# Operands of products at 0 modulo 256, taps for alike placement, and the conditioning dots as one task

## The chip, the cores and the metric

One core of a Trainium2 chip. The time is that of one execution of the program on the device, in microseconds (us); of several runs the median is given. Engines: TensorE (PE) multiplies matrices, VectorE (DVE), ScalarE (ACT) and GpSimd (POOL) work elementwise, SyncE (SP) issues most transfers.

## The reference

A decoder trunk of two layers on 1024 tokens with 1024 channels, in float32. Cut to what matters:

```python
c_act = silu(c)
for i in range(2):
    mod = c_act @ ada_w[i] + ada_b[i]                  # 6 vectors of 1024
    sh_m, sc_m, g_m, sh_f, sc_f, g_f = split(mod, 6)
    h = rms_norm(x, norm_mix_g[i]) * (1 + sc_m) + sh_m
    y = conformer_conv(h, ...) if i == 0 else multiscale_pool(h, ...)
    x = x + (1 + g_m) * y
    h = rms_norm(x, norm_ffn_g[i]) * (1 + sc_f) + sh_f
    x = x + (1 + g_f) * ((silu(h @ w_gate) * (h @ w_up)) @ w_down)   # 1024 -> 2816 -> 1024
return rms_norm(x, final_g)
```

conformer_conv is a product 1024 -> 2048, a GLU, a causal depthwise convolution over 31 tokens (per channel), a layer norm, silu, and a product 1024 -> 1024. multiscale_pool takes means over 2, 4, 8 and 16 tokens and small products.

## The kernel before

Channels lie on the 128 partitions, tokens along the free dimension. The 1024 tokens are two chunks of 512, A and B; the 1024 channels are eight tiles k (or p) of 128. A matrix product in full precision is three products in the one-pass type float32r: both operands are split into a high part and a low rest (`hi`, `lo`), and `products` (L423) does hi x hi, lo x hi and hi x lo into one PSUM bank, each a 128x128 weight and a moving operand of 512 columns.

The program interleaves the chunks: convolution on A, on B, feed-forward of layer 0 on A (the taps of B run beside it), the second convolution product on B, feed-forward of layer 0 on B (pooling of A beside it), and so on, with layer 1. The order of the work is made when the program is built: `unit` lists the units of PE's work, and `pace` (L187) lets tasks issue DVE and POOL instructions where an estimated clock of these engines lags PE's; `finish` (L199) issues a task to its end, there and then. Each engine then runs its own instructions strictly in that order.

**Placement.** The moving operands live in tiles of the pool `slots`. `slot` (L239) gives chunk B a tile of 512 columns. For chunk A it gives a tile of 514 and returns it from column 2 on, since the tile also serves as a buffer of the convolution with two columns ahead (`slot_after`, L243). `wslot` (L247) gives 542 columns (30 of the convolution's past, 512 of the chunk); it holds u, the input of the convolution, later the pooling input hp, and `ffn_p1` (L873) takes the pairs ghi and glo from it. The pool's tiles lie 2080 bytes apart for A, 2048 for B and 2176 for the wide ones. The weights w, two planes of 1024 columns, lie 64 bytes past multiples of 256.

**Taps.** Of the 31 taps of the convolution PE does all for the channel tile p = 7 on chunk A and 8 for p = 6 (`PE_TAPS`, `pe_taps`, L636), as products with diagonal weights; tap j needs u moved by 30 - j tokens, and the moving operand begins at another column for odd and for even taps. `split_u` (L628) makes u's high and low part for p = 6. All other taps are DVE's, or POOL's with ACT (class `Taps`, L660): ca sums DVE's part in PSUM, pa POOL's in SBUF, and the last steps put them together. The layer norm of A then sums the tiles into acc, of which PE takes the mean.

**Dots.** The product c_act @ ada_w is done by DVE: one dot is an instruction over 128x1024 that multiplies a loaded tile adaw (0.5 MB) by c_act and sums along the free dimension. An `ada_task` (L324) holds two buffers, loads ahead over SP's queue, and pauses between dots for a time of `LOAD` (L49, in estimated us of PE). The vectors 4 and 5 of layer 0 (scale and gate of the feed-forward) are two such tasks (L1144), started after the layer norm of A; vector 4 is finished (L1147) ahead of the norm that needs it. The 48 dots of layer 1 start at L1158, with the first feed-forward.

Of the kernel before, what the change touches and what calls it, by code (L numbers as in the profile page):

```python
# [16 lines left out]
P = 128  # L17
D = 1024
S = 1024
KT = D // P  # L20
# [6 lines left out]
PHALO = max(WINDOWS) - 1  # L27
EPS = 1e-6
# [20 lines left out]
LOAD = {"load": 4.0, "slow": 18.0, "next": 4.0, "dots": 3.5}  # L49
# [65 lines left out]
def trunk(ctx, tc, xT, c, vec, ada, adan, w1f, w1, wdg, w2, wgu, wdn, wpl, out):  # L115
# [178 lines left out]


# [28 lines left out]
    def ada_task(l, js, pause=None):  # L324
# [250 lines left out]
    def conv_u(ch, p):  # L575
        u = st["u", ch.i, p] = wslot(ch, "u")
        if ch.i == 0:
            G_.memset(u[:, :HALO], 0.0)
        else:
            G_.tensor_copy(u[:, :HALO], uhalo[:, p, :])  # L580
        return u

    def conv_glu(ch, p, ba, bg):
# [3 lines left out]
        if ch.i == 0 and PE_TAPS.get(p) == CW:  # L587

            V_.scalar_tensor_tensor(ba, ba, V("conv_b1", p), sg, op0=ADD, op1=MUL)
            hi, lo = st["us", p] = [slot_after(A, name) for name in ("uhi", "ulo")]  # L590
            for part in (hi, lo):
                G_.memset(part[:, :2].bitcast(F32), 0.0)
            S_.copy(hi[:, 2:], ba)
            V_.tensor_tensor(lo[:, 2:], ba, hi[:, 2:].bitcast(F32), op=SUB)
# [6 lines left out]
    def conv_in(*todo):  # L601

        def emit(take):
            got = {}
            for each in todo:
# [15 lines left out]
                if ch.i == 0 and 0 < PE_TAPS.get(p, 0) < CW:  # L621
                    split_u(p)
                if ch.i == 0 and PE_TAPS.get(p, 0) < CW:
                    T["taps", 0, p] = Taps(A, p, PE_TAPS.get(p, 0))
# [3 lines left out]
    def split_u(p):  # L628


        u = st["u", 0, p][:, HALO - 2 :]
        hi, lo = st["us", p] = [slot_after(A, name) for name in ("uhi", "ulo")]
# [3 lines left out]
    def pe_taps(p):  # L636

        groups = tap_groups(p)
        us = []
        for i, js in enumerate(groups):  # L640
            def emit(take, i=i, js=js):
# [3 lines left out]
                for q, j in enumerate(js):  # L645
                    o = (CW - 1 - j) // 2 * 2
                    i0 = 2 - (CW - 1 - j) % 2
                    products(b[:, o:], wt, q, [v[:, i0 : i0 + A.n - o] for v in st["us", p]], j == CW - 1, j == CW - PE_TAPS[p])
                    if q % 4 == 3:
                        pace()  # L650
                if i == len(groups) - 1:
                    if PE_TAPS[p] == CW:
# [7 lines left out]
    class Taps:  # L660
# [5 lines left out]
        def __init__(self, ch, p, others=0):  # L666
            self.ch, self.p, self.done, self.urgent = ch, p, False, False
            self.next, self.acc, self.part = 0, None, None

            self.end, self.awaits, self.other = CW - max(others, 1), others > 0, None  # L670
            tasks.append(self)

        def step(self, e):
# [6 lines left out]
            if self.next < self.end:  # L680
                if e == "V" and self.acc is None and sum(isinstance(t, Taps) and t.acc is not None for t in tasks) >= 2:
                    return False
                if e == "G":
                    if self.acc is None and self.part is None and sum(isinstance(t, Taps) and t.part is not None for t in tasks) >= 2:
                        return False
                    if self.next >= self.end - 2:
                        return False
                j = self.next
                self.next += 1
# [21 lines left out]
            d = u[:, HALO : HALO + n]  # L711
            if self.awaits:
                if self.part is not None:
                    V_.tensor_tensor(d, self.part, self.acc, op=ADD)
                else:
                    S_.copy(d, self.acc)
                V_.tensor_tensor(d, d, self.other, op=ADD)
            else:
                if self.part is not None:
                    V_.tensor_tensor(self.acc, self.part, self.acc, op=ADD)  # L720
                V_.scalar_tensor_tensor(d, d, w(CW - 1), self.acc, op0=MUL, op1=ADD)
# [85 lines left out]
    def pool_h(ch, l):  # L807

        hp = st["hp", ch.i] = [wslot(ch, "hp") for _ in range(KT)]
# [63 lines left out]
    def ffn_p1(ch, l, f, pick, first):  # L873
        def emit(take):
# [15 lines left out]
            hi, lo = st["g", ch.i, f] = [wslot(ch, name, F32R)[:, : ch.n] for name in ("ghi", "glo")]  # L890
# [248 lines left out]
    unit(lambda take: finish(*(T["taps", 0, p] for p in range(KT) if PE_TAPS.get(p, 0) < CW)))  # L1139
# [120 lines left out]
```

## Time and profile before

| | us |
|---|---|
| median of 3 runs | 1873.54 (1871.35 to 1875.83) |
| profiled execution | 1871.14 |
| its span, first to last instruction | 1869.4 |
| PE busy | 1826.0 (98%) |
| DVE busy | 990.9 (53%) |
| ACT busy | 968.0 (52%) |
| POOL busy | 614.8 (33%) |

A row of the timeline has the start, the time, the engine, the source line, the operation, what it writes and reads, its shape and count, and in brackets the idle time of the engine just before with what ended it. The time of a product contains its latency and overlaps the next one, so what a product costs PE is the distance from its start to the next start. In a table by stage the numbers are the busy time of PE, PE's weight loads, DVE, ACT and POOL with their counts, the clock that was granted to PE (1.00 is full), and the DMA's share and GB/s. Names such as `hhi`, `ghi`, `vhi`, `mxhi` are high parts of the moving operands of gate and up (and of the first convolution product), of dn, of the second convolution product, and of the pooling product.

### The profile page before, as it was taken

How to read it: one execution, taken by the hardware profiler on the slowest of the kernel's cores; microseconds unless marked ns; L12 is line 12 of the kernel's file. 1: busy time of each engine (PE TensorE's matmuls, PEld its weight loads, DVE VectorE, ACT ScalarE, POOL GpSimd, SP SyncE). 2: the span in 40 equal slices, each digit the busy share in tenths (PEclk: the TensorE clock that was granted, in tenths of full speed). 3: DMA queues.
4: the chain of work that ended last, by engine and by line, in shares of the span. 5: the costliest groups of instructions: out<-in, count | busy, mean ns of one | idle time of the engine just before them, and what ended most of it. 6: DMA issues, size and time to landing. Idle time of an engine off the chain costs nothing.

```text
span 1869.4 us, 21783 instructions
## 1 busy us (share of the span) xinstructions
PE 1826.0 (98%) x8085; PEld 1481.9 (79%) x8085; DVE 990.9 (53%) x1528; ACT 968.0 (52%) x1240; POOL 614.8 (33%) x662
## 2 busy tenths in 40 slices
PE   7999998999999999999999999999999999999997
PEld 5777776888888888877888888888888888888886
DVE  8899856988875235585622233734432233322225
ACT  3775665766656454454644445644534454444443
POOL 4587522877733211272111111511111111111111
PEclk9999998999999999999999999999999999999998
DMA  7958797888978987999887878778778879788782
GB/s 289 300 151 221 172 263 222 225 222 208 223 189 216 231 221 185 283 261 269 227 194 178 211 171 205 182 173 205 181 178 196 192 177 250 176 205 197 181 195 68
DMA packets 108285, 387.56 MB, mean 207 GB/s; under 512 B 11793, under 2 KB 13969, under 8 KB 108178
## 3 DMA queue, kind: packets, MB, share of 16 engines
q0 software_dynamic: 44208, 160.98, 47.2%
q1 hardware_dynamic: 62880, 224.13, 34.6%
q8 instruction: 64, 1.05, 0.2%
q10 hardware_dynamic: 1090, 1.05, 0.2%
q14 instruction: 43, 0.35, 0.1%
HBM read 381.92 MB, written 4.19 MB: 207 GB/s over the span
## 4 chain that ended last, share of the span: by engine, by line
PE 82%; DVE 10%; DMA 6%; issue 1%; ACT 1%; SPq 0%; POOL 0%; DVEq 0%
PE gate L131 24%; PE up L131 24%; PE dn L131 24%; DMA adaw<-in_ada_dram 5%; DVE ca L109 4%; PE y L131 4%; PE first L131 3%; DVE adaw L109 1%; DVE acc L109 1%; PE g L131 1%; PE a L131 1%; DVE x L109 1%; DVE t L109 1%; DMA adaw<-in_adan_dram 1%; DVE hlo L109 1%
## 5 line engine op out<-in xcount | busy, mean ns | idle before, releaser
L109 ACT CAST w<-raw 128x1024 fp32r<-128x1024 f32 x317 | 331.0, 1044 | 508.2 <-issue 303.8
L131 PE MATMUL gate<-hhi,w 128*128 128x512 f32 x1408 | 455.4, 393 | 2.3 <-DVE x L109 1.7
L131 PE MATMUL up<-hhi,w 128*128 128x512 f32 x1408 | 455.9, 393 | 0.0
L131 PE MATMUL dn<-ghi,w 128*128 128x512 f32 (+1 forms) x1440 | 445.7, 386 | 1.2 <-DMA w<-in_wdn_dram 1.2
L417 POOL DMA_DIRECT2D w<-in_wgu_dram x176 | 154.6, 878 | 779.0 <-ACT w L109 759.4
L109 ACT ACTIVATE w<-raw 128x1024 fp32r<-128x1024 f32 x307 | 323.9, 1055 | 0.0
L109 DVE SCALAR_TENSOR_TENSOR x<-dn,gains,x 128x512 f32<-128x512 f32 (+1 forms) x360 | 261.8, 735 | 115.8 <-PE dn L131 115.3
L109 DVE TENSOR_TENSOR t<-t,up 128x512 f32<-128x512 f32 x86 | 59.0, 686 | 495.0 <-PE up L131 474.8
L131 PEld LDWEIGHTS dn<-ghi,w 128*128 128x128 f32 x1440 | 267.9, 188 | 59.8 <-DMA w<-in_wdn_dram 1.6
L131 PEld LDWEIGHTS gate<-hhi,w 128*128 128x128 f32 x1408 | 264.8, 188 | 62.6 <-DVE x L109 2.5
L131 PEld LDWEIGHTS up<-hhi,w 128*128 128x128 f32 x1408 | 264.7, 188 | 59.2 <-DMA w<-in_wgu_dram 0.3
L131 PE MATMUL dn<-glo,w 128*128 128x512 f32 (+1 forms) x720 | 278.7, 387 | 0.0
L131 PE MATMUL gate<-hlo,w 128*128 128x512 f32 x704 | 276.7, 393 | 1.5 <-DVE hlo L109 1.5
L131 PE MATMUL up<-hlo,w 128*128 128x512 f32 x704 | 276.5, 393 | 0.0
L109 POOL TENSOR_TENSOR pa<-pa,pr 128x512 f32<-128x512 f32 x156 | 222.9, 1545 | 13.6 <-ACT pr L109 10.9
L109 DVE SCALAR_TENSOR_TENSOR ca<-u,vecs,ca 128x512 f32<-128x512 f32 x257 | 177.8, 745 | 0.5
L131 PEld LDWEIGHTS gate<-hlo,w 128*128 128x128 f32 x704 | 132.6, 188 | 31.5 <-DVE hlo L109 2.3
L131 PEld LDWEIGHTS dn<-glo,w 128*128 128x128 f32 x720 | 135.2, 188 | 28.1 <-issue 0.2
L131 PEld LDWEIGHTS up<-hlo,w 128*128 128x128 f32 x704 | 132.6, 188 | 29.2
L417 POOL DMA_DIRECT2D w<-in_wdn_dram x88 | 78.3, 890 | 228.4 <-ACT w L109 226.5
L109 DVE SCALAR_TENSOR_TENSOR adaw<-adaw,cact 128x1024 f32<-128x1024 f32 x80 | 118.9, 1488 | 65.1 <-DMA adaw<-in_ada_dram 65.0
L109 ACT ACTIVATE t<-gate 128x512 f32<-128x512 f32 x86 | 51.1, 594 | 157.4 <-PE gate L131 155.4
(145 smaller groups left out, 1776.7 us busy)
## 6 DMA issues: line engine op xcount, KB each, us to landing
raw<-in_wgu_dram SPq DMA_DIRECT2D x176, 512.0 KB, 7.5
w<-in_wgu_dram POOLq DMA_DIRECT2D x176, 512.0 KB, 8.1
raw<-in_wdn_dram SPq DMA_DIRECT2D x88, 512.0 KB, 5.3
w<-in_wdn_dram POOLq DMA_DIRECT2D x88, 512.0 KB, 9.4
adaw<-in_ada_dram SPq DMA_DIRECT2D x64, 512.0 KB, 7.6
raw<-in_w_dram SPq DMA_DIRECT2D x36, 512.0 KB, 6.4
w<-in_w_dram POOLq DMA_DIRECT2D x34, 512.0 KB, 8.5
adaw<-in_ada_dram SPq DMA_DIRECT2D x8, 1024.0 KB, 5.3
```

Of the source, the lines that this page charges most:

```text
L109: self.last = self.order(getattr(self.eng, name)(out, *args, **kw))
L131: last_mm[0] = nc.tensor.matmul(out, lhsT, rhs, start=start, stop=stop).ins.name
L417: order(nc.gpsimd.dma_start(low if len(src.shape) == 2 else low.rearrange("p (a b) -> p a b", a=src.shape[1]), src, accum_op=ADD))
```

## The change

1. *Placement.* A slot of chunk A has 512 columns now. Wide slots come in pairs of 2 x 544 columns (`WSLOT`), half as many; u and hp of two neighbouring channel tiles share a pair, and ghi and glo are the beginning and the end of one. The high and low part of u for p = 7 take a pair of chunk B's. A tile `room` of 48 columns (192 bytes) follows the constants, so that all that lies behind moves by 192 bytes. In the built program the moving operands h, v, mx and g, and all weights w, then begin at multiples of 256 bytes.
2. *Taps of p = 6.* PE takes every second tap from the second-newest back, so that each begins at the same column of the operand and only the output column moves. The newest tap goes to DVE, in the last step as with the other channel tiles. `split_u` runs after the last product of chunk A's first convolution product.
3. *Dots.* The vectors 4 and 5 of layer 0 are one task, started one unit of work earlier (before the last products of B that run beside the layer norm), with a pause of "slow" ahead of the first dot and 4.0 instead of 3.5 between dots. Only vector 4 is finished ahead of the norm; what is left of vector 5 is finished ahead of the fourth unit of the feed-forward, and the dots of layer 1 start there.

The diff, cut to its core:

```diff
+WSLOT = 544
-LOAD = {"load": 4.0, "slow": 18.0, "next": 4.0, "dots": 3.5}
+LOAD = {"load": 4.0, "slow": 18.0, "next": 4.0, "dots": 4.0}
...
-    todo = list(range(CW - 1, CW - 1 - PE_TAPS[p], -1))
+    n = PE_TAPS[p]
+
+    todo = list(range(CW - 1, -1, -1) if n == CW else range(CW - 3, CW - 3 - 2 * n, -2))
...
     def slot(ch, name, dt=F32R):
 
-        return slot_after(ch, name, dt)[:, 2 - 2 * ch.i :]
-
-    def slot_after(ch, name, dt=F32R):
-
-        return slots.tile([P, ch.n + 2 - 2 * ch.i], dt, tag=f"s{ch.i}", name=nm(name))
-
-    def wslot(ch, name, dt=F32):
-
-        return slots.tile([P, ch.width], dt, tag=f"u{ch.i}", name=nm(name), bufs=KT)
+        return slots.tile([P, ch.n], dt, tag=f"s{ch.i}", name=nm(name))
+
+    def wpair(ch, name, dt=F32):
+
+        return slots.tile([P, 2, WSLOT], dt, tag=f"u{ch.i}", name=nm(name), bufs=KT // 2)
+
+    def wslot(ch, name, p):
+
+        if st.get((name, "pair", ch.i), (None,))[0] != p // 2:
+            st[name, "pair", ch.i] = p // 2, wpair(ch, name)
+        return st[name, "pair", ch.i][1][:, p % 2, : ch.width]
+
+    def gslots(ch):
+
+        pair = wpair(ch, "g", F32R)
+        return pair[:, 0, : ch.n], pair[:, 1, WSLOT - ch.n :]
...
+    cst.tile([P, 48], F32, name="room")
...
-                yield pause or ("next" if lax[0] else "slow")
+                yield first if first and i == 0 else pause or ("next" if lax[0] else "slow")
...
-                    o = (CW - 1 - j) // 2 * 2
-                    i0 = 2 - (CW - 1 - j) % 2
-                    products(b[:, o:], wt, q, [v[:, i0 : i0 + A.n - o] for v in st["us", p]], j == CW - 1, j == CW - PE_TAPS[p])
+                    full = PE_TAPS[p] == CW
+                    o = (CW - 1 - j) // 2 * 2 if full else CW - 3 - j
+                    c = j + o if full else 0
+                    products(b[:, o:], wt, q, [v[:, c : c + A.n - o] for v in st["us", p]], j == groups[0][0], j == groups[-1][-1])
...
             d = u[:, HALO : HALO + n]
+            if self.part is not None:
+                V_.tensor_tensor(self.acc, self.part, self.acc, op=ADD)
+            V_.scalar_tensor_tensor(d, d, w(CW - 1), self.acc, op0=MUL, op1=ADD)
             if self.awaits:
-                if self.part is not None:
-                    V_.tensor_tensor(d, self.part, self.acc, op=ADD)
-                else:
-                    S_.copy(d, self.acc)
                 V_.tensor_tensor(d, d, self.other, op=ADD)
...
-            hi, lo = st["g", ch.i, f] = [wslot(ch, name, F32R)[:, : ch.n] for name in ("ghi", "glo")]
+            hi, lo = st["g", ch.i, f] = gslots(ch)
...
+    unit(lambda take: T.__setitem__("ada_f", ada_task(0, (4, 5), "dots", "slow")))
     for p in rest[len(rest) - HOLD - HOLD_LN : len(rest) - HOLD]:
         conv_in((B, p))
     need("ln_a")
-    unit(lambda take: [T.__setitem__(("ada", 0, j), ada_task(0, (j,), "dots")) for j in (5, 4)])
...
-    unit(lambda take: finish(T["ada", 0, 4]))
+    unit(scale_done)
...
-    unit(lambda take: T.__setitem__(("ada", 1), ada_task(1, range(6))))
...
+        if i == GROUP + 1:
+            unit(lambda take: finish(T["ada_f"]))
+            unit(lambda take: T.__setitem__(("ada", 1), ada_task(1, range(6))))
```

`scale_done` issues the steps of the new task until vector 4 is done.

How the instructions move is shown at three places, all on DVE. The first is the end of the sum of squares ahead of the first feed-forward's norm: x_3 is the residual, acc the sum, var and col the steps of the reciprocal root. Before:

```order
L109 SCALAR_TENSOR_TENSOR adaw_2325,mod<-adaw_2325,cact 128x1024
L109 SCALAR_TENSOR_TENSOR x_3_80<-t_2477,gains,x_3_80 128x512
L109 SCALAR_TENSOR_TENSOR adaw_2365,mod<-adaw_2365,cact 128x1024
L109 TENSOR_TENSOR acc_2221<-acc_2221,t_2480 128x512
L109 SCALAR_TENSOR_TENSOR adaw_2368,mod<-adaw_2368,cact 128x1024
L109 TENSOR_SCALAR var_2540<-var_2540 128x4
```

The same place in the changed program:

```order
L113 SCALAR_TENSOR_TENSOR adaw_2380,mod<-adaw_2380,cact 128x1024
L113 TENSOR_TENSOR acc_2202<-acc_2202,t_2410 128x512
L113 SCALAR_TENSOR_TENSOR x_3_80<-t_2447,gains,x_3_80 128x512
L113 TENSOR_TENSOR acc_2202<-acc_2202,t_2450 128x512
L113 SCALAR_TENSOR_TENSOR adaw_2420,mod<-adaw_2420,cact 128x1024
L113 TENSOR_SCALAR var_2508<-var_2508 128x4
```

The dots between and right ahead of the last x and acc are gone; one dot stays ahead of the var steps. In all, 16 dots lie between the layer norm of A and the first gate product before, and 9 now.

The second place follows: the values of the feed-forward's norm (t, then hlo) and the first taps of B (ca), beside the first unit of the feed-forward. Before:

```order
L109 SCALAR_TENSOR_TENSOR t_2603<-x_3_80,gains,rstd_2570 128x512
L109 TENSOR_SCALAR ca_2678<-u_1335,vecs 128x512
L109 SCALAR_TENSOR_TENSOR hlo_2505<-t_2591,mod,hhi_2504 128x512
L109 SCALAR_TENSOR_TENSOR hlo_2507<-t_2595,mod,hhi_2506 128x512
L109 SCALAR_TENSOR_TENSOR hlo_2509<-t_2599,mod,hhi_2508 128x512
L109 SCALAR_TENSOR_TENSOR hlo_2511<-t_2603,mod,hhi_2510 128x512
```

And now:

```order
L113 SCALAR_TENSOR_TENSOR t_2574<-x_3_80,gains,rstd_2541 128x512
L113 SCALAR_TENSOR_TENSOR adaw_2460,mod<-adaw_2460,cact 128x1024
L113 SCALAR_TENSOR_TENSOR hlo_2478<-t_2570,mod,hhi_2477 128x512
L113 TENSOR_SCALAR ca_2654<-u_1330,vecs 128x512
L113 TENSOR_SCALAR ca_2664<-u_1330,vecs 128x512
L113 SCALAR_TENSOR_TENSOR u_1989<-a_2482,vecs,t_2590 128x512
L113 SCALAR_TENSOR_TENSOR hlo_2480<-t_2574,mod,hhi_2479 128x512
L113 SCALAR_TENSOR_TENSOR ca_2654<-u_1330,vecs,ca_2654 128x512
L113 SCALAR_TENSOR_TENSOR adaw_2527,mod<-adaw_2527,cact 128x1024
```

A dot now stands ahead of the last two hlo values, the first taps of B lie between these two, and further dots follow.

The third place is the end of the taps of p = 6 on A, ahead of the layer norm's sum. Before:

```order
L109 SCALAR_TENSOR_TENSOR ca_1742<-u_865,vecs,ca_1742 128x512 x10
L109 TENSOR_TENSOR u_865<-pa_1740,ca_1742 128x512
L109 TENSOR_TENSOR u_865<-u_865,tap_1674 128x512
L109 TENSOR_TENSOR acc_1333<-acc_1333,u_865 128x512
L109 TENSOR_TENSOR acc_1896<-acc_1333,u_993 128x512
```

Now:

```order
L113 SCALAR_TENSOR_TENSOR ca_1736<-u_863,vecs,ca_1736 128x512 x10
L113 TENSOR_TENSOR ca_1736<-pa_1734,ca_1736 128x512
L113 SCALAR_TENSOR_TENSOR u_863<-u_863,vecs,ca_1736 128x512
L113 TENSOR_TENSOR u_863<-u_863,tap_1668 128x512
L113 TENSOR_TENSOR acc_1328<-acc_1328,u_863 128x512
```

One instruction more, the newest tap, stands between the sums and the first acc. PE's instructions keep their order; the eight diagonal taps of p = 6 have other shapes.

More of the change, by code (lines that the diff above doesn't have):

```diff
@@ L322, in ada_load, with ada_task @@
         return w
[L324 removed]
+    def ada_task(l, js, pause=None, first=None):
         def gen():
@@ L660, in trunk, with __init__ @@
     class Taps:
[L666 removed]
+        def __init__(self, ch, p):
             self.ch, self.p, self.done, self.urgent = ch, p, False, False
[L668 to L670 removed]
+            self.acc, self.part, self.other = None, None, None
+            others = tap_groups(p) if ch.i == 0 and p in PE_TAPS else []
+            self.todo, self.awaits = [j for j in range(CW - 1) if not any(j in js for js in others)], bool(others)
             tasks.append(self)
```

43 lines of the change are left out of this document (23 added, 20 removed).

## The prediction

> **What bounds the kernel now.** I read the page first: the span, the share of each engine, the granted clock and the chain.
>
> ```profile
> span 1869.4 us, 21783 instructions
> PE 1826.0 (98%) x8085; PEld 1481.9 (79%) x8085; DVE 990.9 (53%) x1528; ACT 968.0 (52%) x1240; POOL 614.8 (33%) x662
> ...
> PEclk9999998999999999999999999999999999999998
> ...
> PE 82%; DVE 10%; DMA 6%; issue 1%; ACT 1%; SPq 0%; POOL 0%; DVEq 0%
> ```
>
> TensorE (PE) is busy 98% of the span at nearly its full clock, and it carries 82% of the chain. So two things can change the time: how long one product takes, and the few places where PE waits. The groups of products by shape, where they are many:
>
> ```profile
> L131 PE MATMUL up<-hhi,w 128*128 128x512 f32 x1408 | 455.9, 393 | 0.0
> L131 PE MATMUL gate<-hhi,w 128*128 128x512 f32 x1408 | 455.4, 393 | 2.3 <-DVE x L109 1.7 <-ACT hhi L109 0.6
> ...
> L131 PE MATMUL gate<-hlo,w 128*128 128x512 f32 x704 | 276.7, 393 | 1.5 <-DVE hlo L109 1.5
> L131 PE MATMUL up<-hlo,w 128*128 128x512 f32 x704 | 276.5, 393 | 0.0
> ...
> L131 PE MATMUL dn<-ghi,w 128*128 128x512 f32 x1376 | 434.1, 391 | 1.2 <-DMA w<-in_wdn_dram 1.2
> L131 PE MATMUL dn<-glo,w 128*128 128x512 f32 x688 | 269.7, 392 | 0.0
> ```
>
> The two feed-forward layers hold 4224 gate and up products, half for each chunk, and 2064 dn products of 512 columns. The mean of one (390 ns) contains latency. What a product costs PE is the distance between starts, which the timeline gives. In order: one up group of 24 products on chunk A, from its first start to the next group's; eight dn groups of six; one up group of 24 on chunk B.
>
> ```profile
> 329.34 0.40 PE L131 MATMUL up<-hhi,w 128*128 128x512 f32 x1
> ...
> 334.94 0.40 PE L131 MATMUL gate<-hhi,w 128*128 128x512 f32 x1
> ...
> 346.16 0.39 PE L131 MATMUL dn<-ghi,w 128*128 128x512 f32 x1
> ...
> 357.15 0.39 PE L131 MATMUL gate<-hhi,w 128*128 128x512 f32 x1
> ...
> 744.53 0.39 PE L131 MATMUL up<-hhi,w 128*128 128x512 f32 x1
> ...
> 749.97 0.39 PE L131 MATMUL gate<-hhi,w 128*128 128x512 f32 x1
> ```
>
> Chunk A: 5.60 / 24 = 233.3 ns. dn: 10.99 / 48 = 229.0 ns. Chunk B: 5.44 / 24 = 226.7 ns. PE never waits in any of them, the shapes are equal, and so is the arithmetic; the placement of the moving operand differs. In the built program B's h tiles all begin 64 bytes past a multiple of 256, as the weights do. A's, in slots of 514 columns 2080 bytes apart and read from column 2, begin at 8, 40, 72, 104 and so on. The g tiles, 2176 bytes apart, alternate between 64 and 192. Equal placement is fastest, the alternation costs 2.3 ns, and a start that is no multiple of 64 costs 6.7 ns.
>
> The second thing is PE's waits. From 140 to 320 us:
>
> ```profile
> PE var L131 <- DVE acc L109: 5.5, 1, 5.5
> ...
> PE mean L131 <- DVE acc L109: 1.7, 1, 1.7
> PE rstd L131 <- DVE col L109: 1.6, 1, 1.6
> PE gate L131 <- DVE hlo L109: 1.5, 2, 1.4
> ...
> PE gate L131 <- ACT hhi L109: 0.6, 1, 0.6
> ```
>
> All but the mean belong to one place, the norm ahead of the first feed-forward, where VectorE (DVE) works off this:
>
> ```profile
> 293.36 1.22 DVE L109 SCALAR_TENSOR_TENSOR adaw<-adaw,cact 128x1024 f32<-128x1024 f32 x1 [1.81 <-DMA adaw<-in_ada_dram]
> ...
> 294.51 0.75 DVE L109 SCALAR_TENSOR_TENSOR x<-t,gains,x 128x512 f32<-128x512 f32 x1
> ...
> 296.31 0.69 DVE L109 TENSOR_TENSOR acc<-acc,t 128x512 f32<-128x512 f32 x1
> ...
> 300.47 1.22 DVE L109 SCALAR_TENSOR_TENSOR adaw<-adaw,cact 128x1024 f32<-128x1024 f32 x1 [3.47 <-DMA adaw<-in_ada_dram]
> ...
> 307.67 1.23 DVE L109 SCALAR_TENSOR_TENSOR adaw<-adaw,cact 128x1024 f32<-128x1024 f32 x1 [1.93 <-DMA adaw<-in_ada_dram]
> ...
> 308.82 2.72 DVE L109 SCALAR_TENSOR_TENSOR t<-x,gains,rstd 128x512 f32<-128x512 f32 x4
> ```
>
> The adaw rows are the dots of the conditioning weights. DVE reaches each before its data, and the norm's own steps stand behind. From 270 to 310 us such waits sum to:
>
> ```profile
> DVE adaw L109 <- DMA adaw<-in_ada_dram: 19.1, 8, 3.5
> ...
> DMA packets 3217, 11.65 MB, mean 291 GB/s; under 512 B 379, under 2 KB 379, under 8 KB 3214
> ```
>
> **The change, part by part.** *Placement.* All h, v, mx and g operands, and the weights, come to 0 modulo 256. No row has an operand at 0. The nearest rows give the two sides: one more step of 6.7 ns below 226.7 (220.0), and 233.3 above. I take 226.7, because B's row, like the new layout, has both operands of a product and its weights at one offset. The gains:
> - gate and up of chunk A: 2112 x 6.7 ns = 14.1 us. PE never waits there, so all of it counts.
> - dn: 2064 x 2.3 ns = 4.7 us, likewise. The last 96 products, of 256 columns, I leave as they are.
> - chunk A's second convolution product and pooling product, 192 + 48 products: 1.6 us.
> - chunk A's products before 230 us (192 + 192, and the 24 of the short tap group): 408 x 6.7 = 2.7 us. Loads and DVE set the pace there in part, so I count half, 1.4 us; nothing and all are the bounds.
>
> Together 21.8 us. The TensorE page of the Trainium skill ("TensorE: Matmul & The Clock Gate", Back-to-back issue gap) gives N / 2.4 + 2.5 ns, which is 215.8 ns for 512 columns; the trace's best row is 10.9 ns above it. If alignment to 256 closed that distance too, the sum would fall by an estimated 68.5 us more over 6288 feed-forward products.
>
> *Dots.* Nine instead of sixteen stand between the layer norm and the first feed-forward, spaced as far as their loads need. Going by these rows, the stretch on PE is:
>
> ```profile
> 291.19 0.39 PE L131 MATMUL a<-hhi,w 128*128 128x512 f32 x1
> 297.06 1.87 PE L131 MATMUL var<-ones,acc 128*128 128x1 f32 x8 [5.47 <-DVE acc L109]
> 298.79 0.77 PE L131 MATMUL g<-hhi,w 128*128 128x512 f32 x1
> ...
> 303.62 0.63 PE L131 MATMUL g<-hhi,w 128*128 128x512 f32 x1
> 305.89 1.13 PE L131 MATMUL rstd<-ident,col 128*128 128x128 f32 x8 [1.64 <-DVE col L109]
> ```
>
> Without dots in the way x and acc follow their products within some 3 us, before PE is through with its a products at 291.4, so the 5.5 us go. So does the slow stretch behind that wait: from 298.79 to 303.62, eleven distances take 4.83 us (439 ns each) instead of 2.5, 2.3 us. Of rstd's 1.6 us and the 1.7 us by which the dot at 307.67 holds up t, I expect to get back most: the one dot left ahead of the var steps may still wait for its load, for which I keep 1.5 us. Saved: 5.5 + 2.3 + 1.6 + 1.7 - 1.5 = 9.6 us, with bounds of 5 and 11.
>
> The seven dots go on in the feed-forward's first units, one of them ahead of the last hlo values. PE already runs onto hlo there (1.5 us), and a dot of 1.2 us with part of a load wait stands in front: 2 us, between 0 and 9. SP's queue has their loads ahead of weight loads, and a load more every 24 products meets this DMA (its last two numbers are the DMA's share and GB/s):
>
> ```profile
> 324.00:346.00 22.00, 22.00 (x96) 17.76 (x95) 21.52 (x27) 20.21 (x28) 20.67 (x19) 1.00 0.87 219
> ```
>
> One 0.5 MB load in 5.5 us is 95 GB/s more, less 29 for the second layer's load every 18 us, which now starts later: 285 GB/s. The 291 of above shows that the queues can carry that, just.
>
> *Taps of p = 6.* PE takes every second tap, DVE's count stays, but the last tap is now DVE's, one more instruction in the chain that ends with acc ahead of the mean:
>
> ```profile
> 207.42 6.30 DVE L109 SCALAR_TENSOR_TENSOR ca<-u,vecs,ca 128x512 f32<-128x512 f32 x8
> 213.82 0.69 DVE L109 TENSOR_TENSOR u<-pa,ca 128x512 f32<-128x512 f32 x1
> ```
>
> DVE is gapless there and PE waits for it, so 6.30 / 8 = 0.8 us is lost; bounds 0 and 2. The new slots for u and g pair tiles without fewer of them, and the second layer's dots start some 35 us later, with two more left to the forced place in the next unit; PE has no wait for them in the trace, so nothing.
>
> Sum: 21.8 + 9.6 - 2.0 - 0.8 = 28.6 us. The profiled execution took 1871.1 us (span 1869.4 and 1.7 around it), so 1842.5. It was at the fast end of the runs (1871.35 to 1875.83, median 1873.54), so I add 1.5 us for a median: 1844.
>
> **Rivals.** A: 0 modulo 256 is better than 64 modulo 256 for products. For: the trace has steps of 6.7 ns by placement, B's operands are not at a multiple of 256, and a period of 256 shows in the dn row (64 and 192 mixed are dearer than 64 alone). Against: no row shows a product under 226.7. One step less on 6288 products is 41.9 us: 1802. The page's 215.8 would give an estimated 1776.
>
> B, slower: moving operands and weights that begin on one multiple of 256 collide, and every product costs what chunk A's does now. B's gate and up lose 2112 x 6.7 = 14.1 us, dn 2064 x 4.3 = 8.9 us, nothing is gained on A, and the dots still give 6.8: 1873 + 23 - 7 = 1889. It decides once the common distance exceeds some 231 ns. Against: in B's row both already share an offset, at the least cost. The same page of the Trainium skill (Step-by-step) says that weights and moving operand are read by two independent ports; no run here separates them.
>
> C: the seven moved dots choke the DMA at the head of the feed-forward and PE waits for weights or hlo: 9 us given back, 1853.
>
> D: the 6.7 ns do not come from placement but from what else runs beside chunk A (DVE, ScalarE, GpSimd); then only the dots count: 1867. Against: in the second layer a group on chunk A keeps its distance while DVE does nothing at all (the fourth number is DVE's busy time, 0.00):
>
> ```profile
> 1124.31 0.40 PE L131 MATMUL up<-hhi,w 128*128 128x512 f32 x1
> ...
> 1129.91 0.40 PE L131 MATMUL gate<-hhi,w 128*128 128x512 f32 x1
> ```
> ```profile
> 1124.00:1130.00 6.00, 6.00 (x28) 4.84 (x27) 0.00 (x0) 2.49 (x3) 0.89 (x1) 1.00 0.98 217
> ```
>
> Again 5.60 / 24 = 233.3 ns.
>
> **Numbers.** Forecast 53%, A 26%, B 7%, C 10%, D 4%. The forecast's own range, from the bounds of its small terms, is 1836 to 1851. Two in ten may be left out: A reaches below 1802 if more than one step goes, and B lies above, so 1782 to 1858 holds the forecast, C and most of A. 0.2% is 3.7 us, about what a measurement of this kernel can tell from no change. Faster by more: the forecast, A, C and half of D, 0.91. Within: 0.02. Slower: B, 0.07.
>
> **What would show it.** In the changed profile: up groups of 24 on chunk A take 5.44 us from start to start, as on B, and six dn products 1.36; any other number there decides between the forecast, A, B and D. The wait of var for acc is under 1 us, PE's clock stays full behind it, and DVE's waits for adaw from 270 to 310 us fall from 19.1 to under 8. PE waits under 4 us at the first units of the feed-forward, or C is right. I am wrong if B's distance moves from 226.7 at all.

## The result, and the profile after

| | before | after |
|---|---|---|
| median of 4 runs, us | 1872.44 (1870.04 to 1875.83) | 1853.12 (1852.62 to 1860.04) |
| profiled execution, us | 1871.14 | 1852.62 |
| its span, us | 1869.4 | 1850.1 |

The ratio is 0.9904, with a 95% interval of 0.9876 to 0.9933. The kernel is faster by 19.3 us; the forecast was 28.6 us. The time lies inside the wide range that leaves room for rivals, but outside the forecast's own 1836 to 1851. The head of the page of the changed kernel:

```profile
span 1850.1 us, 21796 instructions
PE 1804.3 (98%) x8085; PEld 1481.0 (80%) x8085; DVE 981.8 (53%) x1529; ACT 972.7 (53%) x1247; POOL 621.6 (34%) x661
...
PEclk9999999899999999999999999999999999999998
...
PE 81%; DVE 12%; DMA 6%; issue 1%; ACT 0%; POOL 0%; DVEq 0%; SPq 0%; POOLq 0%; ACTq 0%
```

PE's busy time fell by 21.7 us, from 1826.0. The number of its instructions is the same, so its products became cheaper. The span fell by only 19.3, less than PE's busy time: PE is idle for 45.8 us of it, 43.4 before. DVE's share of the chain went up, from 10 to 12%.

**Placement.** The timeline of PE in the changed kernel: a gate and an up group of chunk A, the start of its dn groups, then an up group and eight dn groups of chunk B.

```profile
322.27 0.39 PE L135 MATMUL gate<-hhi,w 128*128 128x512 f32 x1
...
327.71 0.39 PE L135 MATMUL up<-hhi,w 128*128 128x512 f32 x1
...
333.15 0.39 PE L135 MATMUL dn<-g,w 128*128 128x512 f32 x1
...
744.47 0.39 PE L135 MATMUL up<-hhi,w 128*128 128x512 f32 x1
...
749.91 11.04 PE L135 MATMUL dn<-g,w 128*128 128x512 f32 x48
760.79 0.39 PE L135 MATMUL gate<-hhi,w 128*128 128x512 f32 x1
```

Chunk A: 5.44 and 5.44 us for 24 products, where it was 5.60. dn: 10.88 us for 48, where it was 10.99. Chunk B: 5.44, as before. In each of these groups a product now costs 226.7 ns. Added up over all of PE's products, those beside a wait or at the low clock behind one (below) left out, the distances between starts are 23.4 us shorter. PE's busy time fell by less because the products left out take some 1.7 us more than before.

**The norm ahead of the first feed-forward.** PE's waits from 140 to 320 us, and DVE's wait for the dots' loads from 270 to 310 us:

```profile
PE mean L135 <- DVE acc L113: 3.8, 1, 3.8
PE gate L135 <- DVE hlo L113: 2.7, 3, 1.8
PE y L135 <- POOL vlo L113: 1.8, 1, 1.8
```
```profile
DVE adaw L113 <- DMA adaw<-in_ada_dram: 10.8, 4, 4.2
```

The wait of var (5.5 us) and that of rstd (1.6) are gone. DVE's wait for adaw fell from 19.1 to 10.8 us. On PE the place now reads like this, without an idle time in brackets:

```profile
289.59 0.95 PE L135 MATMUL var<-ones,acc 128*128 128x1 f32 x8
...
293.21 1.05 PE L135 MATMUL rstd<-ident,col 128*128 128x128 f32 x8
...
296.86 0.39 PE L135 MATMUL gate<-hhi,w 128*128 128x512 f32 x1
```

**The mean of A's layer norm.** Here the wait grew, from 1.7 to 3.8 us, and something follows it that did not follow the shorter wait:

```profile
213.32 2.08 PE L135 MATMUL mean<-acc,ones 128*128 128x512 f32 x2 [3.79 <-DVE acc L113]
...
216.90 0.63 PE L135 MATMUL a<-hlo,w 128*128 128x512 f32 x1
...
218.18 0.63 PE L135 MATMUL a<-hlo,w 128*128 128x512 f32 x1
```

From 216.90 to 218.18 lie three products: 427 ns each, where they are 227 ns apart before the wait and again from 219.7 us on. Behind this wait PE runs at about half speed for some microseconds.

**The first dn group.** This is where the forecast was given back. PE's waits from 300 to 360 us, and their places on PE's timeline:

```profile
PE dn L135 <- DVE t L113: 4.0, 1, 4.0
PE dn L135 <- DVE x L113: 2.2, 1, 2.2
PE gate L135 <- DVE hlo L113: 2.1, 2, 1.8
```
```profile
344.10 2.93 PE L135 MATMUL dn<-g,w 128*128 128x512 f32 x6 [3.99 <-DVE t L113]
349.22 4.61 PE L135 MATMUL dn<-g,w 128*128 128x512 f32 x12 [2.19 <-DVE x L113]
```

DVE at that time, and the issue on SP's queue of the load that DVE waits for:

```profile
332.32 1.62 DVE L113 SCALAR_TENSOR_TENSOR adaw<-adaw,cact 128x1024 f32<-128x1024 f32 x1
...
340.89 1.23 DVE L113 SCALAR_TENSOR_TENSOR adaw<-adaw,cact 128x1024 f32<-128x1024 f32 x1 [5.61 <-DMA adaw<-in_ada_dram]
...
343.36 0.68 DVE L113 TENSOR_TENSOR t<-t,up 128x512 f32<-128x512 f32 x1
...
348.42 2.06 DVE L113 SCALAR_TENSOR_TENSOR x<-dn,gains,x 128x512 f32<-128x512 f32 x3
```
```profile
328.31 0.33 SPq L145 DMA_DIRECT2D adaw<-in_ada_dram  x1
```

The dot at 340.89 is the last of vector 5, issued by the forced `finish` ahead of the first dn group. Its load was issued at 328.31, as soon as the buffer came free, and landed 12.6 us later. DVE stood before it for 5.6 us. In its queue behind stand t<-t,up, which frees the PSUM bank of the third up group (PE waits 4.0 us for that), and x<-dn, which frees the banks of dn (2.2 us). The windows show the DMA full just then (last two numbers: DMA share, GB/s), and the clock behind the wait (the number before them):

```profile
336.00:340.00 4.00, 4.00 (x19) 3.07 (x17) 0.00 (x0) 2.36 (x3) 1.62 (x2) 1.00 1.06 303
340.00:354.00 14.00, 7.83 (x21) 5.67 (x21) 13.11 (x20) 5.25 (x8) 11.41 (x11) 0.63 0.60 172
```

Where the time went is seen best from the starts of the same PE instructions (us, from each timeline; PE's order is the same in all of them, except around the first dn group in `dn_later_16`, where the fifth pair is in the same place again). `old_dots`, `new_dots_only` and `dn_later_16` are experiments, below.

| start of | before | after | old_dots | new_dots_only | dn_later_16 |
|---|---|---|---|---|---|
| rstd of A's layer norm | 232.39 | 231.74 | 233.53 | 234.26 | 232.75 |
| first gate product | 310.37 | 296.86 | 314.79 | 300.41 | 297.80 |
| gate of the fifth pair | 368.34 | 364.57 | 371.15 | 369.19 | 358.26 |
| a gate product of B, layer 0 | 752.46 | 741.52 | 748.11 | 753.30 | 735.64 |
| A's pooling product | 891.19 | 883.31 | 883.78 | 898.97 | 876.91 |
| last product | 1861.50 | 1842.98 | 1843.06 | 1869.29 | 1836.71 |

Between rstd and the first gate product the changed kernel wins 12.9 us on the one before. From there to the fifth pair it loses 9.7 of them, although placement saves over 1 us there. Between 741 and 883 us it loses another 3.1. The rest is placement: 7.2 us from the fifth pair to the fourth row, 10.6 us behind the pooling product.

Each column is one execution. Up to the first gate product eight of the versions below issue the same instructions as the changed kernel, with operands and weights alike, and that product starts anywhere from 295.4 (`dn_later`) to 300.7 us (`at32`) in them. So a difference of a few us between two starts says little by itself. The length of a stretch repeats better: from rstd to the first gate product they all take 65.1 to 66.0 us.

### The profile page after: what moved, and what is told of

Read it like the earlier page. It is cut to its first block, busy times and chain, and to the rows that moved or that the text cites. A ratio compares the mean times of both kernels' runs of the same rounds, so it can differ in the third digit from the quotient of the medians.

```text
span 1850.1 us, 21796 instructions
## 1 busy us (share of the span) xinstructions
PE 1804.3 (98%) x8085; PEld 1481.0 (80%) x8085; DVE 981.8 (53%) x1529; ACT 972.7 (53%) x1247; POOL 621.6 (34%) x661
## 4 chain that ended last, share of the span: by engine, by line
PE 81%; DVE 12%; DMA 6%; issue 1%; ACT 0%; POOL 0%; DVEq 0%; SPq 0%; POOLq 0%; ACTq 0%
PE dn L135 23%; PE up L135 23%; PE gate L135 23%; PE y L135 6%; DMA adaw<-in_ada_dram 5%; DVE ca L113 4%; PE first L135 3%; DVE adaw L113 2%; PE a L135 1%; DVE acc L113 1%; PE g L135 1%; DVE t L113 1%; DVE x L113 1%; DVE hlo L113 1%; PE rstd L135 1%
## 5 line engine op out<-in xcount | busy, mean ns | idle before, releaser
L135 PE MATMUL dn<-g,w 128*128 128x512 f32 (+1 forms) x2160 | 492.2, 387 | 8.3 <-DVE t L113 4.0
L135 PEld LDWEIGHTS dn<-g,w 128*128 128x128 f32 x2160 | 400.4, 189 | 91.4 <-DVE t L113 4.4
L135 PE MATMUL gate<-hhi,w 128*128 128x512 f32 x1408 | 450.7, 389 | 2.5 <-DVE x L113 2.5
L135 PE MATMUL up<-hhi,w 128*128 128x512 f32 x1408 | 451.3, 390 | 0.0
L113 POOL TENSOR_TENSOR pa<-pa,pr 128x512 f32<-128x512 f32 x163 | 235.0, 1552 | 18.3 <-ACT pr L113 15.9
L113 DVE SCALAR_TENSOR_TENSOR ca<-u,vecs,ca 128x512 f32<-128x512 f32 x249 | 173.5, 745 | 0.3
L113 DVE SCALAR_TENSOR_TENSOR adaw<-adaw,cact 128x1024 f32<-128x1024 f32 x80 | 111.4, 1394 | 68.3 <-DMA adaw<-in_ada_dram 68.3
L113 ACT ACTIVATE pr<-u,vecs 128x512 f32<-128x512 f32 x163 | 109.9, 714 | 38.2 <-DVE u L113 16.0
L113 DVE TENSOR_TENSOR g<-t,g 128x512 fp32r<-128x512 f32 x70 | 61.6, 880 | 64.7 <-ACT g L113 64.7
```

Source lines behind the costliest of these rows:

```text
L113: self.last = self.order(getattr(self.eng, name)(out, *args, **kw))
L135: last_mm[0] = nc.tensor.matmul(out, lhsT, rhs, start=start, stop=stop).ins.name
```

## The experiments

**1 and 2. The two halves apart.** `old_dots` takes part 3 back; `new_dots_only` puts part 3 alone into the kernel before.

```diff
 # old_dots, against the changed kernel; new_dots_only is the reverse in the kernel before
-LOAD = {"load": 4.0, "slow": 18.0, "next": 4.0, "dots": 4.0}
+LOAD = {"load": 4.0, "slow": 18.0, "next": 4.0, "dots": 3.5}
...
-    unit(lambda take: T.__setitem__("ada_f", ada_task(0, (4, 5), "dots", "slow")))
...
+    unit(lambda take: [T.__setitem__(("ada", 0, j), ada_task(0, (j,), "dots")) for j in (5, 4)])
...
-    unit(scale_done)
+    unit(lambda take: finish(T["ada", 0, 4]))
...
+    unit(lambda take: T.__setitem__(("ada", 1), ada_task(1, range(6))))
     taps(B, *range(KT))
...
-        if i == GROUP + 1:
-            unit(lambda take: finish(T["ada_f"]))
-            unit(lambda take: T.__setitem__(("ada", 1), ada_task(1, range(6))))
```

> The changed kernel with part 3 taken back: the vectors 4 and 5 are two tasks again, started after the layer norm of A, pause 3.5, and layer 1's dots start with the feed-forward. Placement and taps stay changed. Theory G (given back: the new schedule of the dots wins some 13 us at the norm and loses some 11 us at the first dn group, where VectorE waits for a dot's load): 1850 to 1857, no more than 4 us from the changed kernel; the wait of var for acc ahead of the feed-forward is back at some 5 us, and the wait of dn for t at 340 us is gone. Rival H (the schedule gains as forecast and the lost time lies elsewhere): 1860 to 1863. Rival I (the new schedule costs more than it brings): 1840 to 1848.

> The kernel before with part 3 alone: one task, started one unit earlier, pause 4.0, vector 5 finished ahead of the fourth unit of the feed-forward. Placement and taps are as before. Theory G: 1868 to 1874, within 4 us of the kernel before, with a gain of some 10 us up to the first gate product and a loss of some 10 us at the first dn group. Rival H: 1862 to 1865, the 6.8 to 7.6 us of the forecast.

Measured: old_dots 1851.84 us, ratio to the kernel before 0.9889 (0.9868 to 0.9910), which cannot be told from the changed kernel. new_dots_only 1875.6 us, ratio 1.0019 (1.0004 to 1.0034). So part 3 gains nothing that these runs can tell, neither beside the new placement nor without it, and the 19 us come from parts 1 and 2. No run has the taps of part 2 alone; the distances between products put the gain on the placement. Theory G is right in its places, and in size for old_dots; new_dots_only came out 1.6 us above the range that G gave. In old_dots the waits of the norm are back; from 140 to 300 us:

```profile
PE var L135 <- DVE acc L113: 6.8, 1, 6.8
```

In the table old_dots reaches the first gate product 17.9 us behind the changed kernel, the fifth pair only 6.6 behind, and the pooling product 0.5 behind: what the new schedule wins at the norm is paid back at two places, 11 us at the first dn group and 6 us between 741 and 883 us. The second place I had not expected. It is no chance of one execution: new_dots_only loses 6.9 us in this stretch on the kernel before, and the next two runs, at64 and at32, lose 6.4 and 6.9 on old_dots. So it comes with part 3.

**3 and 4. Is it the multiple of 256, of 64, or that all lie alike?** Only the size of `room` changes, so that every operand and weight moves alike; all instructions stay.

```diff
 # at64
-    cst.tile([P, 48], F32, name="room")
 # at32
-    cst.tile([P, 48], F32, name="room")
+    cst.tile([P, 40], F32, name="room")
```

> The changed kernel without the 192 bytes of the tile room: every operand and every weight then begins 64 bytes past a multiple of 256, instead of at the multiple; all instructions and their order are the same. Theory M (a start at a multiple of 64 is all that counts): no difference, 1850 to 1856, products 226.7 ns apart. Rival N (a multiple of 256 is worth something): more than 4 us slower, products over 227.3 ns apart.

> The changed kernel with room at 160 instead of 192 bytes: every operand and every weight begins at 224 modulo 256, which is 32 modulo 64; all alike, and all instructions and their order are the same. Theory M (multiple of 64): every product of 512 columns costs 6.7 ns more, 7536 x 6.7 = 50 us, of which the few places that wait take some: 1895 to 1904, products 233.3 ns apart. Rival E (operands need only lie alike, or in a fixed distance to the weights): 1850 to 1856, products 226.7 ns apart.

Measured: at64 1854.21 us, ratio 0.9896 (0.9869 to 0.9923); at32 1854.77, ratio 0.9899 (0.9876 to 0.9921). Rival N fell with at64, and theory M with at32: at 32 modulo 64 nothing is lost. An up group of at32:

```profile
1389.99 0.39 PE L135 MATMUL up<-hhi,w 128*128 128x512 f32 x1
...
1395.43 0.39 PE L135 MATMUL gate<-hhi,w 128*128 128x512 f32 x1
```

5.44 us, 226.7 ns a product. The `room` of the change does nothing that these runs can tell. Operands and weights lie alike in all three, at 0, 64 and 224 modulo 256.

**5. Weights and operands apart.** Everything stays where it is in the changed kernel, but the weights begin 32 bytes later.

```diff
     cst.tile([P, 48], F32, name="room")
+    wts.tile([P, 8], F32, name="gap", bufs=1)
```

> The changed kernel with a tile of 32 bytes ahead of the weights: the moving operands stay at 0 modulo 256, every weight begins at 32 modulo 256; the order of all instructions is the same. In the kernel before, too, chunk A's operands did not lie as the weights do. Theory W (what counts is that operand and weights begin at the same place modulo 64): products 233.3 ns apart, 7536 x 6.6 = 50 us, 1895 to 1904. Rival S (only the moving operands count, among themselves or by their own start): products 226.7 ns apart, 1850 to 1857.

Measured: 1892.81 us, ratio 1.0117 (1.0101 to 1.0134). An up group, then the eight dn groups behind it:

```profile
609.94 0.40 PE L135 MATMUL up<-hhi,w 128*128 128x512 f32 x1
...
615.54 0.40 PE L135 MATMUL dn<-g,w 128*128 128x512 f32 x1
...
626.74 0.40 PE L135 MATMUL gate<-hhi,w 128*128 128x512 f32 x1
```

5.60 / 24 and 11.20 / 48 are both 233.3 ns. The operands still begin at 0 modulo 256 and are all alike, so only their distance to the weights can be what costs; the weights' own start is no multiple of 64, but neither is it in at32. Theory W holds in that the distance counts; that it counts modulo 64 does not, as the next runs show. The time is some us under its 1895. A likely reason is that waits hide part of the dearer products: rstd of A's layer norm starts at 231.79 us here and at 231.74 in the changed kernel.

**6 to 8. Which distances cost.** Only g moves: glo by 128 bytes on both chunks (`glo128`); chunk A's ghi and glo both by 8, with everything else as in at64 (`g_off8`); chunk A's glo by 192 and chunk B's ghi by 64 (`mixed`).

```diff
 # glo128
-        return pair[:, 0, : ch.n], pair[:, 1, WSLOT - ch.n :]
+        return pair[:, 0, : ch.n], pair[:, 1, : ch.n]
 # g_off8, chunk A, in a pair of 2 x 576 columns, without room
+        s = 2 if ch.i == 0 else 0
+        return pair[:, 0, s : s + ch.n], pair[:, 1, s : s + ch.n] if s else pair[:, 1, WSLOT - ch.n :]
 # mixed
+        if ch.i == 0:
+            return pair[:, 0, : ch.n], pair[:, 1, 16 : 16 + ch.n]
+        return pair[:, 0, 16 : 16 + ch.n], pair[:, 1, WSLOT - ch.n :]
```

> The changed kernel with glo at the beginning of its half of the pair: ghi at 0, glo at 128 modulo 256, as ghi and glo lay 128 apart in the kernel before. Same instructions and order. Theory R (a product costs more where its operand begins at another place modulo 256 than its neighbour's): dn products 229.0 ns apart as before, 2064 x 2.3 = 4.7 us, 1856 to 1860. Rival O (what counts is each operand's own start, which here is a multiple of 64 throughout): dn 226.7, 1850 to 1856.

> The changed kernel without room (operands at 64 modulo 256) and with chunk A's ghi and glo begun two columns later, so all of them at 72 modulo 256, which is 8 modulo 32; chunk B's stay at 64. Same instructions and order. Theory O (a start that is no multiple of 32 costs, whatever the neighbours): chunk A's 1056 dn products of 512 columns 232 to 234 ns apart, 6 to 7 us, 1858 to 1863; chunk B's 226.7. Rival R (only a change of the start from one product to the next costs): all dn 226.7, 1850 to 1856.

> The changed kernel with g placed at two further distances from the weights, which stay at 0 modulo 256: chunk A's glo at 192 (two of each six dn products), chunk B's ghi at 64 (four of each six), the rest at 0. Same instructions and order on TensorE. Theory D (a product of 512 columns costs 233.3 instead of 226.7 ns wherever its operand and its weights do not begin at the same place modulo 256): six dn products take 1360 + 2 x 6.7 = 1373 ns on chunk A and 1360 + 4 x 6.7 = 1387 ns on chunk B; 1704 x... in all 352 x 6.7 + 672 x 6.7 = 6.8 us, so 1857 to 1862. Rival F (distances of 64 and 192 are free, only 128 and those that are no multiple of 64 cost): 1360 ns on both chunks, 1850 to 1856.

Measured: glo128 1858.41 us, ratio 0.9928 (0.9911 to 0.9946); g_off8 1862.58, ratio 0.9959 (0.9944 to 0.9974); mixed 1864.05, ratio 0.9973 (0.9955 to 0.9990). The first and the next-behind row of eight dn groups each, in glo128; in g_off8 on chunk A, then on B; in mixed on A, then on B:

```profile
508.02 0.39 PE L135 MATMUL dn<-g,w 128*128 128x512 f32 x1
...
519.01 0.39 PE L135 MATMUL gate<-hhi,w 128*128 128x512 f32 x1
```
```profile
1382.58 0.40 PE L135 MATMUL dn<-g,w 128*128 128x512 f32 x1
...
1393.79 0.39 PE L135 MATMUL gate<-hhi,w 128*128 128x512 f32 x1
...
1646.94 0.39 PE L135 MATMUL dn<-g,w 128*128 128x512 f32 x1
...
1657.82 0.39 PE L135 MATMUL gate<-hhi,w 128*128 128x512 f32 x1
```
```profile
1381.46 0.39 PE L135 MATMUL dn<-g,w 128*128 128x512 f32 x1
...
1392.46 0.39 PE L135 MATMUL gate<-hhi,w 128*128 128x512 f32 x1
...
1646.45 0.40 PE L135 MATMUL dn<-g,w 128*128 128x512 f32 x1
...
1657.65 0.40 PE L135 MATMUL gate<-hhi,w 128*128 128x512 f32 x1
```

glo128: 10.99 / 48 = 229.0 ns, the dn row of the kernel before. g_off8: 11.21 / 48 = 233.5 on A, 10.88 / 48 = 226.7 on B; neighbours there are alike, so a change between neighbours is not needed for the cost, and R alone falls. In glo128 rival O falls, and with it a period of 64: a distance of 128 costs. In mixed rival F falls. mixed: 11.00 / 48 = 229.2 on A, as D has it (1373 / 6 = 228.9), but 11.20 / 48 = 233.3 on B, where D has 231.1: there all six products cost the 6.7 ns, the two of glo at distance 0 as well. D's count falls a second time in the kernel before, whose groups with ghi (four of six products) and those with glo (two of six) at distance 128 both took about 229. So: all at one place modulo 256 costs 226.7; one distance of 8 or 32 throughout costs 233.3; how the cost of mixed distances adds up is open.

**9. The stall at the first dn group.** The group goes behind the fourth pair of gate and up groups, and the forced end of vector 5 with it.

```diff
     fa = ffn(A, 0, False)
+    fa[3], fa[4] = fa[4], fa[3]
...
-        if i == GROUP + 1:
+        if i == GROUP + 2:
```

> The changed kernel with the first dn group of chunk A's first feed-forward put behind the fourth gate and up pair instead of ahead of it, and the forced end of vector 5 with it: the last dots get some 11 us more. Theory G (the gain at the norm is given back since VectorE waits 5.6 us for the last dot's load ahead of the first dn updates): dn's waits of 4.0 and 2.2 us and the slow products behind them go, 9 to 11 us less: 1842 to 1846. Rival Q (the queues are full there anyway, so the wait moves along with the work): 1850 to 1856, with a wait of 4 us or more in the same stretch.

Measured: 1850.66 us, ratio 0.9888 (0.9869 to 0.9907). That cannot be told from the changed kernel, but half of theory G came true. The waits of PE for t and x at the first dn group are gone, although DVE still waits 4.7 us for a dot's load at 339.78, and the fifth pair starts at 355.74 instead of 364.57, 8.8 us earlier, of which it had 1.5 at the first gate product. But from 770 to 800 us there is a new wait:

```profile
PE rstd L135 <- DVE col L113: 6.3, 1, 6.3
```

It takes back the greater part: the last row but one of the table would read 879.28, only 4.0 us ahead of the changed kernel.

There is a second sign that this load sets the stall. In at32, with the instructions of the changed kernel, the last dot's load was issued at 332.16 and took 8.9 us instead of 12.6. DVE then waits less:

```profile
341.10 1.43 DVE L113 SCALAR_TENSOR_TENSOR adaw<-adaw,cact 128x1024 f32<-128x1024 f32 x1 [1.99 <-DMA adaw<-in_ada_dram]
```

From the first gate product to the fifth pair at32 takes 62.7 us, against 67.7 in the changed kernel and 60.3 in dn_later.

**10 and 11. The dots of layer 1.** Within the feed-forward they start some 35 us later in the changed kernel, 11 more in dn_later. A shorter pause between them, alone (`layer1_16`) and with dn_later (`dn_later_16`):

```diff
-LOAD = {"load": 4.0, "slow": 18.0, "next": 4.0, "dots": 4.0}
+LOAD = {"load": 4.0, "slow": 18.0, "layer1": 16.0, "next": 4.0, "dots": 4.0}
...
-                yield first if first and i == 0 else pause or ("next" if lax[0] else "slow")
+                yield first if first and i == 0 else pause or ("next" if lax[0] else "layer1")
```

> The changed kernel with a pause of 16 instead of 18 between the dots of layer 1 alone, so that its 24th dot comes some 48 us earlier, which makes up for the start that the change put some 35 us later. Theory L (the later start leaves more dots to the forced places ahead of the pooling, where they hold up VectorE at the norm of chunk B and its weights: the changed kernel loses some 3 us on the kernel before between 760 and 870 us, and the variant with the later dn group some 10 us there): the lead holds through that stretch, 1848 to 1852. Rival K (denser dots take the transfers from the weights all along): 1853 to 1860.

> The first dn group and the forced end of vector 5 one gate and up pair later, together with the pause of 16 in layer 1. Theory L with G: the wait of 6.3 us of rstd for col at 780 us that the later dn group alone brought is gone, and with it 8 to 10 us: 1838 to 1844. Rival K: no more than the later dn group alone, 1848 to 1853.

Measured: layer1_16 1852.68 us, ratio 0.9903 (0.9882 to 0.9924), no gain over the changed kernel. dn_later_16 1843.28 us, ratio 0.9850 (0.9830 to 0.9870), 9.8 us under the changed kernel and the fastest version here. Its only wait of rstd from 700 to 800 us:

```profile
PE rstd L135 <- DVE col L113: 1.6, 1, 1.6
```

G is shown by this at its place: with the first dn group out of the way of the last dot, the stretch from the first gate product to the fifth pair takes 60.3 us in dn_later and 60.5 in dn_later_16, and most of the gain at the norm stays. Theory L does not hold as put. In layer1_16 the lead still shrinks between 741 and 883 us, and the dots in that stretch are about as many in every version (26 to 28 from 740 to 900 us). What differs is how long DVE waits for their loads from 740 to 860 us (14.9 us before, 21.6 in old_dots, 27.9 in new_dots_only, 35 to 40 in the changed kernel, dn_later, layer1_16, dn_later_16 and taps12) and whether one of these waits falls just ahead of the norm's col. That is read from the traces; no run separates it, and the cause at this place stays open.

**12. The mean.** PE takes 12 instead of 8 taps of p = 6.

```diff
-PE_TAPS = {6: 8, 7: CW}
+PE_TAPS = {6: 12, 7: CW}
```

> The changed kernel with 12 instead of 8 taps of p = 6 on PE: 12 more products of 2.7 us in all ahead of the mean, one more 0.5 MB load, and four taps less for VectorE or GpSimd. Theory V (VectorE alone sets when the mean can start; PE's lead of 5.7 us runs into it, waits 3.8 us, and the slow clock behind so long a wait costs 2 to 3 us more): the wait falls under 2 us, no products over 400 ns behind it, 1848 to 1852. Rival P (the extra products and the load cost what the wait gives): 1852 to 1856.

Measured: 1853.16 us, ratio 0.9903 (0.9882 to 0.9924): no gain in the end, as rival P has it. At the place itself theory V holds:

```profile
211.12 1.10 PE L135 MATMUL mean<-acc,ones 128*128 128x512 f32 x2 [1.59 <-DVE acc L113]
...
212.29 0.40 PE L135 MATMUL a<-hlo,w 128*128 128x512 f32 x1
212.52 0.40 PE L135 MATMUL a<-hhi,w 128*128 128x512 f32 x1
```

The products behind the shorter wait are 230 ns apart, not 427, and the first gate product starts at 294.06, 2.8 us earlier than in the changed kernel, although PE has 12 products more. The gate product of B in the fourth row is still 2.4 us earlier, at 739.13; between there and the pooling product (883.66) the lead is lost, at the same open place as above. Leads of this size also arise between two executions of the same instructions; the shorter wait is the firmer sign, since in the changed kernel and in the eight versions with the same instructions up to there this wait is 3.8 to 3.9 us.

## Why the prediction was right, and where it was wrong

*Placement, 21.8 us: right.* The distances give 23.4, each group has the predicted length, and B's distance did not move from 226.7. That rules out A, B and D of the rivals, and at64 shows the same for 0 against 64 modulo 256. The reason chosen ("Equal placement is fastest") was the right one of the two that the text gave; the other ("a start that is no multiple of 64 costs 6.7 ns") is wrong: at32 has such starts and pays nothing, and w32 has none among its moving operands and pays everywhere. What counts is the distance to the weights. The Trainium skill's page "SBUF — State Buffer" (Operand start alignment) speaks of what is legal and says that its runs timed nothing; these runs time it, at 6.7 ns in 226.7. No group of products here came near the 215.8 ns that the formula in the section Back-to-back issue gap of the Trainium skill's page "TensorE: Matmul & The Clock Gate" gives: 226.7 is the least that any of these runs shows for an undisturbed group. That PE's busy time fell by 21.7, almost the forecast figure, is partly luck: slow products took back what placement gave beyond it.

*Dots at the norm, 9.6 us: right in mechanism, too small.* From rstd to the first gate product 12.9 us were won, of which A's 192 products of the second convolution are 1.3; the other 11.6 lie just above the bound of 11. Some 0.9 us of that are the eight products of var, which had run slow as well (213 ns apart, 112 now). DVE's waits for adaw fell to 10.8 us, not under 8 as forecast, but none of them held up PE.

*The seven dots in the first units, 2.0 us with bounds of 0 and 9: this step failed.* The loss was 9.7 us, about 11 without the placement gain in that stretch. The step looked at the dot ahead of the last hlo, and there it was nearly right (2.1 us of waiting against 1.5 before). It did not follow the forced end of vector 5 to its place: the last dot is issued whether its load is there or not, ahead of the x updates and the t that free PSUM, and the DMA that "can carry that, just" needed 12.6 us for the load. at32, where this load took 8.9 us, lost 5 us less. That is rival C's place and its 9 us, by another way than the waits of PE for weights or hlo that it named; its 1853 is the measured time, and the forecast's own test (PE's waits at the first units under 4 us, "or C is right") decided for it with 8.3 us. The stated range held because it was wide enough for the rivals, C among them.

*The last tap ahead of the mean, 0.8 us: not seen as such.* The wait grew by 2.1 us, and the slow products behind it cost some 2 more. But new_dots_only, which has the taps and the placement of the kernel before, waits 3.9 us there as well, so the moved tap is not needed for it. PE comes to the mean 5.7 us earlier than before: by placement, and because in the profiled execution before it had waited 1.8 us for another load at 177 us, with eight products 427 ns apart behind that. DVE sets the start of the mean, and that is only 3.6 us earlier. taps12 is in line with this; what the one tap costs no run shows.

*The later dots of layer 1, nothing: wrong.* Between 741 and 883 us the changed kernel loses 6 us on old_dots, and it is part 3 that brings this. That it has to do with the dots' waits is likely, their number does not explain it, and the cause is open.

The sum by the traces: 0.7 us won up to rstd (less than two executions differ by), 12.9 at the norm, -9.7 at the first units, 7.2, -3.1, and 10.6 us behind the pooling product make 18.5 us, the difference of the two profiled executions.

## What to carry to other kernels

Compare the start-to-start distance of products of equal shape; where it differs, look at where the moving operands lie against the weights modulo 256, and place them alike, wherever that is. Work that is moved out of one wait has a deadline somewhere else: follow it to the instruction that forces it, and ask what stands behind that in the engine's queue and whether its load can be there. A lead on one engine is worth nothing at a place where another sets the start, and can be worth less than nothing where the clock is low behind the wait.

## What the runs showed of the hardware

- 512-column products in float32r cost 226.7 ns (5.44 us for 24) where operand and weights begin at the same place modulo 256 (tried at 0, 64 and 224), 233.3 ns (5.60 us) at a distance of 32 bytes and 233.5 at one of 8. One operand in three at a distance of 128 or 192 costs 229.0 and 229.2 on average; two in three at 64 cost 233.3.
- At the mean, waits of 1.6 and 1.7 us left PE at full speed (distances of 230 ns right behind), and a wait of 3.8 us was followed by products 427 ns apart for some 5 us; so was the one of 4.0 us at the first dn group. The length of the one wait does not decide it alone. Ahead of the first gate<-hlo both the changed kernel and layer1_16, with the same instructions up to there, wait 1.8 us: the first goes on with products some 235 ns apart, the second soon has some 427 ns apart:

```profile
310.74 0.50 PE L135 MATMUL gate<-hlo,w 128*128 128x512 f32 x1 [1.81 <-DVE hlo L113]
...
312.11 0.63 PE L135 MATMUL up<-hhi,w 128*128 128x512 f32 x1
312.54 0.63 PE L135 MATMUL gate<-hhi,w 128*128 128x512 f32 x1
```

In at32 a wait of 2.8 us at the first dn group left the granted clock at 1.00. The Trainium skill's page "TensorE: Matmul & The Clock Gate" (Part 1: The HAM clock gate) says that an idle window of about 3.4 us halves the clock, and that such a product takes 426.7 ns then. The traces agree with the 426.7 ns; in layer1_16 a wait of 1.8 us was enough.

- With the DMA's share at 1.06 (303 GB/s) a load of 0.5 MB took 12.6 us from issue to use, against a median of 8.1 us from issue to landing for these loads from 200 to 350 us.
